# Norm squares on VectorE, later Gelus, deferred gate products and a shifted route in a one-core PEER decoder block

## The chip, the cores and the metric

The kernel runs on one core of a Trainium2 chip. The core has TensorE (PE, with its weight loads PEld), VectorE (DVE), ScalarE (ACT) and GpSimd (POOL), SyncE (SP), which here only issues transfers, and 16 DMA engines that serve all queues. The metric is device time in microseconds (us); lower is better. Times are the median of repeated runs; one further execution was profiled, and all rows of the trace are from that one.

## The reference

The layer is a decoder block on 512 tokens of width 1024, in float32: a mixer of two recurrent head groups, a cross-attention on 256 memory tokens, then a PEER layer, each behind an RMSNorm and added to the stream, and a last RMSNorm. The change lies in the PEER layer and the norm behind it. PEER picks, for each token and each of 8 heads, 16 of 128×128 experts by two sets of 128 keys, and sums the experts' outputs:

```python
def peer_ffn(h, wq, sub_keys, u_table, v_table):
    ...
    q = (hf @ wq).reshape(t, PEER_HEADS, 2, PEER_HALF)
    sc = jnp.einsum('thpd,hpnd->thpn', q, sub_keys).astype(jnp.float32)
    top_v, top_i = lax.top_k(sc, PEER_TOPK)
    ...
    best_v, best_pos = lax.top_k(cand, PEER_TOPK)
    expert_id = jnp.take_along_axis(cand_id, best_pos, axis=-1)
    gate = jax.nn.softmax(best_v, axis=-1)
    ...
    def block(args):
        xb, eb, gb = args
        u = jnp.take(u_table, eb, axis=0)
        act = jax.nn.gelu(jnp.einsum('phkd,pd->phk', u, xb).astype(jnp.float32), approximate=False)
        wgt = (gb * act).astype(v_table.dtype)
        return jnp.einsum('phk,phkd->pd', wgt, jnp.take(v_table, eb, axis=0))
```

So each token uses 128 rows of `u_table` and 128 of `v_table`, of 1024 floats each.

## The kernel before, in words

The 512 tokens are four tiles of 128. The PEER layer is computed in two ways at the same time.

*Gathered tiles* (two tiles, `G0`). `peer_gather` is a generator; each step is one row of work for 128 tokens: POOL gathers one `u` row for each token (`fetch`, L1066, 512 KB), and VectorE multiplies it with the token's vector and sums (L1093). 128 such rows give a tile's 128 activations. A tile's activations then go through Gelu on ScalarE and a product with the gates on VectorE (`weights_`, L1073 and L1074); in the code this is called in the middle of the next 128 rows. Then 128 `v` rows per tile are gathered and added up with those weights (L1104). The order is: 128 `u` rows of the first tile, 128 of the second, 128 `v` rows of the first, 128 of the second, 512 in all, numbered 1 to 512 here. `close` adds the residual to a finished tile, squares it (L1083), takes the norm and returns it for its store; the first tile is closed in the middle of the last 128 rows, the second at the very end. The rows land in a ring of buffers (`buffer`), 14 of them late in the kernel.

*Dense tiles* (two tiles, `G1`). For these all 16384 experts are computed. They are cut into 128 blocks of 128 experts; block e needs 512 KB of each table. For a block, PE multiplies the `u` block with the 256 tokens (L313), ScalarE applies Gelu from PSUM into a room in SBUF (`act_`, L965), VectorE multiplies with the gates of eight blocks at a time (`gated`, L990), and PE multiplies with the `v` block into four PSUM banks that stay open over all blocks (`add`, L993). The `u` side runs 47 blocks ahead (`AHEAD`): 47 blocks are done before the dense loop (`ahead`, called by the letter `a` of the order below), and the other 81 inside it, so at loop step e the activation is that of block e+47. Steps 0 to 80 have both halves, steps 81 to 127 the `v` half alone. The activation's PSUM pool has two banks.

*Gates of the dense tiles.* `route` finds a tile's experts: per head a top 16 of 50 candidates, then the indices are turned by comparisons in float16 (`key`, `at`, `hit`, `prod`). Each `yield` is a step: candidates, eight heads, the rest. `build` then makes, for 16 tokens, the table of gates for all experts: one-hot rows on VectorE (L934), their product with the gates (L938), a product of one-hots on PE (L943), a copy to a staging tile on ScalarE (L944). 14 of 16 groups of the staging tile are stored to DRAM and loaded by POOL later (`gates_of`, L985); the first two groups (`NOW`) are multiplied in place into the activations at once by VectorE (L949). There are 16 builds, eight per dense tile, and three staging tiles.

The order in which the parts are emitted is the string `ORDER_XA`, read from left to right: `p5` runs five steps of the gather, `t2` and `T2` two steps of the route of the first and second dense tile, `b1` and `B1` one build, `a1` one block ahead. 158 gather rows are emitted before the dense loop. In the dense loop `ROWS_BOTH` rows are emitted per step while both halves run and `ROWS_DOWN` afterwards; what is left runs behind the loop. The order of emission isn't the order of an engine's queue: that is set when the program is compiled, by a planner that takes for each engine what its estimate says is ready, the earlier emitted first. Each engine then works its queue strictly in order. Waits between engines are semaphores.

Of the kernel before, what the change touches and what calls it, by code (L numbers as in the profile page):

```python
# [11 lines left out]
AF = mybir.ActivationFunctionType  # L12
OP = mybir.AluOpType
# [15 lines left out]
K = 16  # L29
NSL = PH * K  # L30

ROWS_BOTH, ROWS_DOWN = 3.5, 1.65
NKEY = 128

GSCALE = 2.0 ** 15
# [20 lines left out]
ORDER_XA = ("w2 n0 q008 n1 s0 x0 s1 x1 q104 o0 w1 i0 q148 f0 f1 r6 "  # L56
            "f2 s2 p2 f3 s3 p4 x2 p3 r3 p2 r3 k0 x3 p4 o1 p8 i1 e0 R3 p4 R3 p2 R4 k1 "
            "u0 p5 u1 p5 u2 p5 a1 u3 p5 a2 "
            + "t2 p4 a1 " * 4 + "t2 p4 a9 " + "b1 p5 a1 T2 " * 4 + "b1 p5 a1 T2 a7 d0 " + "b1 p5 a2 " * 3
            + "B1 p5 a1 " * 6 + "a1 p9 B1 p5 B1 p5 a6 ")  # L60


class Phase:
# [12 lines left out]
def _body(ctx, tc, A, out, dbg):  # L76
    from contextlib import ExitStack
    nc = tc.nc
    V, SC, PE, G = nc.vector, nc.scalar, nc.tensor, nc.gpsimd
# [706 lines left out]
    class Peer:  # L786
# [50 lines left out]
        def route_(self, i, spot, hs, PH):  # L837

            tvv = self.tv[i].rearrange("p (a b) c -> p a b c", b=2)[:, hs]
            cand = sct.tile([P, PH, NCAND], F32, name="cand")  # L840
            bv, bi, idf = self.bv[i][:, hs], self.bi[i][:, hs], self.idf[i][:, :, hs]
            tix = self.tix[i][:, 2 * hs.start:2 * hs.stop]
            off = 0
            for a0, n, w in RECT:
                o = cand[:, :, off:off + n * w].rearrange("p h (a b) -> p h a b", a=n)
                G.tensor_tensor(o, tvv[:, :, 0, a0:a0 + n].unsqueeze(3).to_broadcast([P, PH, n, w]),
                                tvv[:, :, 1, 0:w].unsqueeze(2).to_broadcast([P, PH, n, w]), op=OP.add)
                off += n * w
            yield
            for h in range(PH):  # L850
                topk(sct, cand[:, h], bv[:, h], bi[:, h], NCAND)
                yield


            key = sct.tile([P, PH, 2, K], F16, name="key")
            SC.activation(key.rearrange("p a b c -> p (a b) c"), tix, AF.Copy)
            at = sct.tile([P, PH, K], F16, name="at")
            SC.activation(at, bi, AF.Copy)
            step = sct.tile([P, PH, K], F16, name="step")
            V.tensor_copy(step[:, :, 0:1], key[:, :, 0, 0:1])  # L860
            V.tensor_tensor(step[:, :, 1:], key[:, :, 0, 1:], key[:, :, 0, :K - 1], op=OP.subtract)
            hit, prod = (x[:, :PH] for x in spot())
            shape = [P, PH, K, K]

            def over(x):
                return x.unsqueeze(1).to_broadcast(shape)

            def total(out):
                n = K // 2
                while n > 1:  # L870
                    V.tensor_tensor(prod[:, :, :n], prod[:, :, :n], prod[:, :, n:2 * n], op=OP.add)
                    n //= 2
                V.tensor_tensor(out, prod[:, :, 0], prod[:, :, 1], op=OP.add)
            V.tensor_tensor(hit, at.unsqueeze(2).to_broadcast(shape), over(rows_[:, 0]), op=OP.is_ge)
            V.tensor_tensor(prod, hit, step.unsqueeze(3).to_broadcast(shape), op=OP.mult)
            total(idf[:, 0])
            V.tensor_tensor(prod, hit, over(rows_[:, 1]), op=OP.mult)
            first = sct.tile([P, PH, K], F16, name="first")
            total(first)
            V.tensor_tensor(first, at, first, op=OP.subtract)  # L880
            V.tensor_tensor(hit, first.unsqueeze(2).to_broadcast(shape), over(rows_[:, 2]), op=OP.is_equal)
            V.tensor_tensor(prod, hit, key[:, :, 1].unsqueeze(3).to_broadcast(shape), op=OP.mult)
            total(idf[:, 1])
            if self.ids[i] is not None:
                V.scalar_tensor_tensor(self.ids[i][:, hs], idf[:, 0], float(P), idf[:, 1], op0=OP.mult, op1=OP.add)
            yield
# [32 lines left out]
    TG, TS = 16, 8  # L919
    GB = 8  # L920
    NOW = 2
# [5 lines left out]
    def build(t0, bufs, stage, bank):  # L927

        for s in range(0, TG, TS):
            ts = slice(t0 + s, t0 + s + TS)  # L930
            oj, oi, og = hot(bufs())
            key = [slot[:, x, ts].rearrange("p (a q) -> p a q", q=Q).unsqueeze(2) for x in range(2)]
            for o, k in ((oj, key[1]), (oi, key[0])):
                V.tensor_tensor(o, ioq.unsqueeze(1).to_broadcast([P, TS // Q, P, Q]),  # L934
                                k.to_broadcast([P, TS // Q, P, Q]), op=OP.is_equal)
            gates = slot[:, 2:4, ts].rearrange("p g (a q) -> p g a q", q=Q)
            for a in range(TS // Q):
                V.tensor_tensor(og[:, :, a], oi[:, a].unsqueeze(1).to_broadcast([P, 2, P, Q]),  # L938
                                gates[:, :, a].unsqueeze(2).to_broadcast([P, 2, P, Q]), op=OP.mult)
                ps = bank()  # L940
                for k in range(Q):
                    for g in range(2):
                        PE.matmul(ps[:, k], oj[:, a, :, k], og[:, g, a, :, k], start=g == 0, stop=g == 1)  # L943
                SC.activation(stage[:, :, s + a * Q:s + a * Q + Q], ps.rearrange("p t i -> p i t"), AF.Copy, scale=1.0 / GSCALE)  # L944
        nc.scalar.dma_start(gates_[:, :, t0 // TG].rearrange("g p i t -> p g (i t)"),
                            stage[:, NOW * GB:].rearrange("p (g i) t -> p g (i t)", i=GB))
        for g in range(NOW):
            a = room[g][:, :, t0:t0 + TG]
            V.tensor_tensor(a, a, stage[:, g * GB:(g + 1) * GB], op=OP.mult)  # L949

    NHOT = TS * 4 * P

# [6 lines left out]
    room, count_a = [], [0]  # L959
# [102 lines left out]
    def peer_gather(ready, buffer):  # L1062

        def fetch(table, ids, s):
            row = buffer()
            G.indirect_dma_start(out=row, out_offset=None, in_=A[table],  # L1066
                                 in_offset=bass.IndirectOffsetOnAxis(ap=ids[:, s:s + 1], axis=0))
            return row
        late_ = NSL // 2

        def weights_(ti):

            SC.activation(act[ti], act[ti], AF.Gelu)  # L1073
            V.tensor_tensor(act[ti], act[ti], ready[ti], op=OP.mult)  # L1074

        def close(ti):
            hn = first.hn[ti]
            x, wr, junk = buffer(), buffer(), buffer()
            G.dma_start(x, out[ti * P:(ti + 1) * P, :])
            row_(4, wr, G)  # L1080
            V.tensor_tensor(hn, hn, x, op=OP.add)
            ss = sm.tile([P, 1], F32, name="nss")
            SC.activation(junk, hn, AF.Square, accum_out=ss)  # L1083
            V.scalar_tensor_tensor(hn, hn, rstd(ss, 1, "n", 1.0 / D), wr, op0=OP.mult, op1=OP.mult)
            return out[ti * P:(ti + 1) * P, :], hn

        act, done, stored = {}, [], []
        for ti in G0:
            act[ti] = per.tile([P, NSL], F32, name=f"act{ti}", bufs=1)
            hn, ids = first.hn[ti], first.ids[first.tiles.index(ti)].rearrange("p a b -> p (a b)")  # L1090
            for s in range(NSL):
                row = fetch("pu", ids, s)
                V.scalar_tensor_tensor(row, row, 1.0, hn, op0=OP.mult, op1=OP.mult, accum_out=act[ti][:, s:s + 1])  # L1093
                if s == late_ and done:
                    weights_(done.pop())
                yield
            done.append(ti)
        for ti in G0:
            hn, ids = first.hn[ti], first.ids[first.tiles.index(ti)].rearrange("p a b -> p (a b)")
            for s in range(NSL):  # L1100
                row = fetch("pv", ids, s)
                w = act[ti][:, s:s + 1]
                if s:
                    V.scalar_tensor_tensor(hn, row, w, hn, op0=OP.mult, op1=OP.add)  # L1104
                else:
                    V.tensor_scalar(hn, row, w, None, op0=OP.mult)
                if s == late_:
                    if ti == G0[0]:
                        weights_(done.pop())
                    else:  # L1110
                        stored.append(close(G0[0]))
                if s == late_ + 32 and stored:
                    G.dma_start(*stored.pop())
                yield
        G.dma_start(*close(G0[1]))

    mixer(tuple(range(NT)), memory_kv)
# [73 lines left out]
    for what in ORDER_XA.split():  # L1191
# [50 lines left out]
        else:  # L1242
            if kind not in flows:
                i, f = {"r": (0, 0), "R": (1, 0), "t": (0, 0), "T": (1, 0), "b": (0, 1), "B": (1, 1)}[kind]
                g = first if kind in "rR" else second
                flows[kind] = settle(g, g.tiles[i]) if f else g.route(g.tiles[i], spot, 2 if kind == "r" else 1)
            run(flows[kind], n)
    assert count_a[0] == AHEAD
    pe.close()
    pss.close()  # L1250
    wu = pool("wu", 1, side="right")
# [67 lines left out]
```

## Time and profile before

| | us |
|---|---|
| median of 3 runs | 1926.71 (1925.36 to 1937.04) |
| the profiled execution | 1930.96 |
| its span, first to last instruction | 1929.0 |
| PE busy | 1686.6 |
| VectorE busy | 1244.0 |
| GpSimd busy | 839.0 |
| ScalarE busy | 397.8 |

The kernel moves 514.81 MB. A row of the profile's slices cuts the span in 40 parts of 48.2 us; a digit is a tenth of the slice. In the list of waits a line gives the engine and line that waited, for whom, the total, how often, and the longest. A line such as `x40: 383/383/384, 1361.3 to 1629.9` counts instructions of one kind, with shortest, median and longest in ns and the first and last start in us. PE's busy time is that of overlapping records; how fast it goes is read from the distance of starts.

### The profile page before, as it was taken

To read this page: it belongs to the slowest core of one execution; us is meant where nothing else is said; L and a number is where in the kernel's file an instruction comes from. 1 tells how busy PE (TensorE), PEld (TensorE's weight loads), DVE (VectorE), ACT (ScalarE), POOL (GpSimd) and SP (SyncE) were. 2 spreads that over 40 slices of the span, in tenths; PEclk is the share of its full clock that TensorE was granted. 3 is DMA by queue.
4 is the path that set the end of the run, shared out by engine and by line. 5 is a ranking of instruction groups with operands and counts; after the bars stand their busy time and mean duration, and the time that the engine had idled before them with its cause. 6 is when DMAs were issued, how large, how long until landed. Compare 5 with 4: busy or idle time off the path is not lost.

```text
span 1929.0 us, 21360 instructions
## 1 busy us (share of the span) xinstructions
PE 1686.6 (87%) x7444; PEld 1245.9 (65%) x7444; DVE 1244.0 (64%) x2753; ACT 397.8 (21%) x798; POOL 839.0 (43%) x686
## 2 busy tenths in 40 slices
PE   5999999999799978978997699974999999239997
PEld 3878778777788847867886466643666666125443
DVE  5656754662523898997896956668566665797611
ACT  5443442752442222112222100000000000000000
POOL 2122111332210255571543746568566666676500
PEclk9999999999899988998998799986999999669999
DMA  3111111234534678887899999999999999999962
GB/s 133 61 55 55 45 50 56 66 112 150 178 118 147 230 278 305 321 322 254 298 357 350 345 385 410 410 410 392 410 410 409 410 410 410 403 408 410 409 208 87
DMA packets 165355, 514.81 MB, mean 267 GB/s; under 512 B 15616, under 2 KB 44416, under 8 KB 163456
## 3 DMA queue, kind: packets, MB, share of 16 engines
q0 software_dynamic: 76608, 286.30, 38.3%
q1 hardware_dynamic: 59712, 212.48, 30.2%
q10 hardware_dynamic: 28928, 14.68, 2.6%
q8 instruction: 58, 0.95, 0.2%
q14 instruction: 49, 0.40, 0.1%
HBM read 494.52 MB, written 18.87 MB: 266 GB/s over the span
## 4 chain that ended last, share of the span: by engine, by line
PE 42%; DMA 26%; DVE 20%; issue 5%; POOL 4%; ACT 2%; DVEq 0%; SPq 0%; POOLq 0%; ACTq 0%
PE o L993 9%; PE pj L271 7%; DMA row<-in_pv,ids 7%; PE pj L313 6%; PE pj L284 6%; PE acc L445 4%; DMA W<-in_pv,ids 3%; DVE dh L1104 3%; PE acc L943 3%; DVE W L1093 2%; DMA wl<-in_pu,ids 2%; DMA row<-in_pu,ids 2%; DMA W<-in_pu,ids 2%; DMA Vm<-in_pu,ids 2%; DMA KT<-in_pv,ids 2%
## 5 line engine op out<-in xcount | busy, mean ns | idle before, releaser
L313 PE MATMUL pa<-dh,ld 128*128 128x256 f32 x1296 | 299.5, 385 | 105.2 <-ACT dh L965 104.6
L993 PE MATMUL o<-ld,W 128*128 128x512 f32 x832 | 369.9, 595 | 2.1 <-DVE W L949 1.1
L313 PEld LDWEIGHTS pa<-dh,ld 128*128 128x128 f32 x1296 | 250.2, 194 | 174.1 <-ACT dh L965 106.3
L993 PEld LDWEIGHTS o<-ld,W 128*128 128x128 f32 x832 | 158.9, 191 | 174.1 <-issue 167.4
L221 POOL TENSOR_TENSOR wl<-w,wh 128x1024 fp32r<-128x1024 f32 x38 | 92.4, 2434 | 343.9 <-ACT wh L236 289.7
L313 PE MATMUL pj<-dh,w 128*128 128x256 f32 x704 | 167.8, 393 | 4.5 <-ACT W L965 4.5
L313 PEld LDWEIGHTS pj<-dh,w 128*128 128x128 f32 x704 | 137.1, 199 | 23.2 <-ACT W L965 4.9
L1066 POOL DMA_INDIRECT W<-in_pu,ids x71 | 94.4, 1329 | 97.1 <-DVE W L1093 44.5
L1066 POOL DMA_INDIRECT row<-in_pu,ids x74 | 97.4, 1316 | 83.1 <-DVE row L1093 36.9
L1104 DVE SCALAR_TENSOR_TENSOR dh<-row,act,dh 128x1024 f32<-128x1024 f32 x72 | 92.5, 1284 | 57.2 <-DMA row<-in_pv,ids 56.4
L1066 POOL DMA_INDIRECT row<-in_pv,ids x74 | 99.7, 1348 | 47.0 <-DMA W<-in_pv,ids 20.1
L313 PE MATMUL pj<-dh 128*128 128x256 f32 x496 | 111.4, 380 | 1.8 <-ACT W L965 1.8
L1093 DVE SCALAR_TENSOR_TENSOR row<-row,dh 128x1024 f32<-128x1024 f32 x74 | 89.1, 1220 | 36.3 <-DMA row<-in_pu,ids 36.0
L284 PE MATMUL pj<-hT,wh 128*128 128x512 f32 x320 | 110.9, 418 | 0.0
L965 ACT ACTIVATE W<-pa 128x256 f32<-128x256 f32 x65 | 24.9, 383 | 401.9 <-PE pa L313 396.4
L271 PE MATMUL pj<-wh,hT 128*128 128x512 f32 x320 | 106.3, 405 | 0.4 <-ACT hT L211 0.4
L313 PEld LDWEIGHTS pj<-dh 128*128 128x128 f32 x496 | 93.7, 191 | 14.3 <-ACT W L965 2.2
L1093 DVE SCALAR_TENSOR_TENSOR W<-W,dh 128x1024 f32<-128x1024 f32 x71 | 86.0, 1222 | 15.5 <-DMA W<-in_pu,ids 15.4
L993 PE MATMUL o<-ld,dh 128*128 128x512 f32 x192 | 85.2, 593 | 0.0
L236 ACT ACTIVATE wh<-w 128x1024 fp32r<-128x1024 f32 x56 | 59.3, 1058 | 124.7 <-PE pj L271 64.1
L1066 POOL DMA_INDIRECT wh<-in_pu,ids x41 | 64.3, 1567 | 33.2 <-DVE wh L1093 8.5
L1066 POOL DMA_INDIRECT wl<-in_pu,ids x42 | 49.8, 1186 | 66.1 <-DVE tv L783 18.6
(431 smaller groups left out, 3090.3 us busy)
## 6 DMA issues: line engine op xcount, KB each, us to landing
ld<-in_pv SPq DMA_DIRECT2D x128, 512.0 KB, 6.8
ld<-in_pt SPq DMA_DIRECT2D x81, 512.0 KB, 6.8
gates__132<-W ACTq DMA_DIRECT2D x16, 896.0 KB, 12.3
W<-gates__132 POOLq DMA_DIRECT2D x14, 1024.0 KB, 17.4
w<-in_pt SPq DMA_DIRECT2D x24, 512.0 KB, 6.8
dh<-in_pt SPq DMA_DIRECT2D x23, 512.0 KB, 6.9
w<-in_win SPq DMA_DIRECT2D x20, 512.0 KB, 3.6
w<-in_pwq SPq DMA_DIRECT2D x16, 512.0 KB, 4.0
```

Of the source, the lines that this page charges most:

```text
L221: G.tensor_tensor(out, a, hi, op=OP.subtract)
L236: SC.activation(hi, wt, AF.Copy)
L271: PE.matmul(acc[i], a[:, d, i * P:(i + 1) * P], b[:, z], start=d == 0 and m == 0, stop=d == DB - 1 and m == len(pairs) - 1)
L284: PE.matmul(acc[:, :n * P], a[:, d], b[:, d], start=d == 0 and m == 0, stop=d == DB - 1 and m == 2)
L313: PE.matmul(ps, w[:, d], h[:, d], start=d == 0, stop=d == DB - 1)
L445: PE.matmul(ps[:, i], l[:, i], r[:, i], start=True, stop=True)
L943: PE.matmul(ps[:, k], oj[:, a, :, k], og[:, g, a, :, k], start=g == 0, stop=g == 1)
L965: SC.activation(place(e), ps, AF.Gelu)
L993: PE.matmul(outs[DENSE[i]][z], place(e)[:, i * P:(i + 1) * P], v[:, z * 512:(z + 1) * 512], start=e == 0, stop=e == NKEY - 1)
L1066: G.indirect_dma_start(out=row, out_offset=None, in_=A[table], in_offset=bass.IndirectOffsetOnAxis(ap=ids[:, s:s + 1], axis=0))
L1093: V.scalar_tensor_tensor(row, row, 1.0, hn, op0=OP.mult, op1=OP.mult, accum_out=act[ti][:, s:s + 1])
L1104: V.scalar_tensor_tensor(hn, row, w, hn, op0=OP.mult, op1=OP.add)
```

## The change

It has six edits, which keep the computation.

1. `close` squares on VectorE (an operation with a running sum) in place of ScalarE's Square.
2. `weights_` is called at the 121st row of the next 128 rows in place of the 65th; `close` of the first tile stays at the 65th.
3. `build` hands its two products for the first two groups to a list, and the next build runs them in its second half, between the one-hots and their products with the gates. The last is run behind the order string.
4. `route_` converts the indices and positions to float16 on VectorE in place of ScalarE.
5. In the order string two steps of the second dense tile's route and four gather rows stand ahead of the first build; the later ones move up, and a `p9` near the end becomes `p5`.
6. `ROWS_BOTH` is 3.15 in place of 3.5, `ROWS_DOWN` 2.3 in place of 1.65.

```diff
-ROWS_BOTH, ROWS_DOWN = 3.5, 1.65
+ROWS_BOTH, ROWS_DOWN = 3.15, 2.3
...
-            + "t2 p4 a1 " * 4 + "t2 p4 a9 " + "b1 p5 a1 T2 " * 4 + "b1 p5 a1 T2 a7 d0 " + "b1 p5 a2 " * 3
-            + "B1 p5 a1 " * 6 + "a1 p9 B1 p5 B1 p5 a6 ")
+            + "t2 p4 a1 " * 4 + "t2 p4 a9 T2 p4 " + "b1 p5 a1 T2 " * 4 + "b1 p5 a8 d0 " + "b1 p5 a2 " * 3
+            + "B1 p5 a1 " * 6 + "a1 p5 B1 p5 B1 p5 a6 ")
...
-            SC.activation(key.rearrange("p a b c -> p (a b) c"), tix, AF.Copy)
+            V.tensor_copy(key.rearrange("p a b c -> p (a b) c"), tix)
             at = sct.tile([P, PH, K], F16, name="at")
-            SC.activation(at, bi, AF.Copy)
+            V.tensor_copy(at, bi)
...
             gates = slot[:, 2:4, ts].rearrange("p g (a q) -> p g a q", q=Q)
+            while s and fresh:
+                fresh.pop()()
             for a in range(TS // Q):
...
-        for g in range(NOW):
-            a = room[g][:, :, t0:t0 + TG]
-            V.tensor_tensor(a, a, stage[:, g * GB:(g + 1) * GB], op=OP.mult)
+
+        def apply():
+            for g in range(NOW):
+                a = room[g][:, :, t0:t0 + TG]
+                V.tensor_tensor(a, a, stage[:, g * GB:(g + 1) * GB], op=OP.mult)
+        fresh.append(apply)
+
+    fresh = []
...
-        late_ = NSL // 2
+        late_, later = NSL // 2, NSL - 8
...
-            SC.activation(junk, hn, AF.Square, accum_out=ss)
+            V.scalar_tensor_tensor(junk, hn, 1.0, hn, op0=OP.mult, op1=OP.mult, accum_out=ss)
...
-                if s == late_ and done:
+                if s == later and done:
                     weights_(done.pop())
...
-                if s == late_:
-                    if ti == G0[0]:
-                        weights_(done.pop())
-                    else:
-                        stored.append(close(G0[0]))
+                if s == later and ti == G0[0]:
+                    weights_(done.pop())
+                if s == late_ and ti != G0[0]:
+                    stored.append(close(G0[0]))
...
     assert count_a[0] == AHEAD
+    fresh.pop()()
     pe.close()
```

## The prediction

> **What bounds the kernel now.** I read the page first (busy time, slices), then a table of stretches, then the waits inside the stretches where PE falls idle, then ScalarE in order of time.
>
> ```profile
> span 1929.0 us, 21360 instructions
> PE   5999999999799978978997699974999999239997
> PEclk9999999999899988998998799986999999669999
> GB/s 133 61 55 55 45 50 56 66 112 150 178 118 147 230 278 305 321 322 254 298 357 350 345 385 410 410 410 392 410 410 409 410 410 410 403 408 410 409 208 87
> ...
> 620.00:864.00 244.00, 214.29 (x964) 175.04 (x962) 222.06 (x944) 46.03 (x109) 123.41 (x118) 0.94 0.79 285
> 885.00:1108.00 223.00, 188.82 (x1061) 162.13 (x1060) 188.17 (x380) 53.26 (x102) 102.47 (x72) 0.91 0.90 316
> ...
> 1288.00:1327.00 39.00, 0.71 (x2) 0.00 (x0) 34.68 (x56) 0.50 (x3) 30.20 (x25) 0.55 1.02 404
> 1327.00:1638.00 311.00, 310.87 (x1076) 207.02 (x1077) 192.17 (x149) 17.59 (x47) 203.48 (x154) 0.99 1.02 408
> 1638.00:1720.00 82.00, 15.94 (x54) 9.76 (x52) 69.08 (x54) 1.33 (x4) 58.74 (x54) 0.62 1.02 406
> 1754.00:1845.00 91.00, 91.00 (x214) 40.41 (x213) 58.07 (x56) 1.53 (x3) 47.83 (x36) 1.00 1.00 396
> 1845.00:1929.00 84.00, 73.84 (x173) 32.44 (x171) 8.47 (x22) 2.89 (x8) 0.54 (x1) 0.97 0.38 123
> ...
> 1632.00:1929.00 297.00, 220.63 (x571) 110.19 (x570) 171.04 (x168) 8.03 (x20) 135.29 (x115) 0.88 0.84 323
> ```
>
> A window row gives its stretch, its length, busy time of PE, PEld, DVE, ACT and POOL (with counts), the granted clock, the DMA share and GB/s. From 1108 us to 1845 us DMA moves about 400 to 410 GB/s whatever PE does: that stage is DMA's. After 1845 us DMA is nearly empty (123 GB/s) while PE is still busy 73.84 of 84 us. So PE arrives late at the end, with work that could have run earlier, beside full transfers. It lost that time in two holes, 1288 to 1327 and 1638 to 1720, where it was idle while DMA ran on. Before 1108 us DMA is not full, and VectorE is the busiest of what remains: 222.06 of 244 and 188.17 of 223 us.
>
> The waits in the two holes:
>
> ```profile
> ACT act L1073 <- DVE row L1093: 54.6, 1, 54.6
> PE pa L313 <- ACT dh L965: 38.4, 1, 38.4
> ...
> ACT row L1083 <- DVE dh L1081: 81.5, 1, 81.5
> PE pa L313 <- ACT dh L965: 66.2, 1, 66.2
> ...
> 1052.73 0.30 ACT L1073 ACTIVATE act<-act 128x128 f32<-128x128 f32 x1
> 1058.77 0.38 ACT L965 ACTIVATE W<-pa 128x256 f32<-128x256 f32 x1
> ...
> L965 ACT ACTIVATE W<-pa x25: 383/383/383, 1058.8 to 1257.8; 128x256 f32<-128x256 f32 x25
> L965 ACT ACTIVATE dh<-pa x2: 383/383/383, 1264.7 to 1271.5; 128x256 f32<-128x256 f32 x2
> ...
> L965 ACT ACTIVATE W<-pa x40: 383/383/384, 1361.3 to 1629.9; 128x256 f32<-128x256 f32 x40
> L965 ACT ACTIVATE dh<-pa x7: 365/383/384, 1326.7 to 1636.8; 128x256 f32<-128x256 f32 x7
> ...
> L965 ACT ACTIVATE dh<-pa x7: 363/383/383, 1719.7 to 1754.1; 128x256 f32<-128x256 f32 x7
> ...
> 600.00:1637.00 1037.00, 549.15 (x407) 0.94 0.93 353
> 600.00:1718.60 1118.60, 605.74 (x456) 0.91 0.94 357
> ```
>
> ScalarE works its queue in order. The square of the first gathered tile's norm (L1083) stands in it behind 74 of the 81 dense activations (25+2+40+7), and can't run before VectorE has reached row 449 of the 512 gathered rows. PE runs on to that point at 6.89 us a block ((1629.9−1361.3)/39), but the rows come more slowly: only 407 had been issued at 1637 us. So ScalarE stood 81.5 us for the square, the next activations stood behind it, the two PSUM banks stayed full, and PE lost 66.2 us. The first hole is the same with the Gelu of the second tile's activations (L1073), which needs row 256 and stands behind 27 dense activations.
>
> The last two rows, and those below of the gathers, are windows of L1066 alone, in which x counts rows issued. The queue orders aren't those of the source: the first L1073 is emitted at row 193, some ten blocks into the dense loop (158 rows stand ahead of it), but ran at 1052.73 us, ahead of the first dense activation; the second is emitted at row 321, block 46, and ran behind block 26. An activation goes where the planner of the program thought its input ready.
>
> **The change part by part.** The rows of the end come first: PE's last stretch, and the closing of the second gathered tile.
>
> ```profile
> 1835.58 83.27 PE o L993 x194
> ...
> 1839.81 1.23 DVE L1081 TENSOR_TENSOR dh<-dh,W 128x1024 f32<-128x1024 f32 x1 [1.12 <-DMA W<-out]
> 1844.56 1.28 DVE L1084 SCALAR_TENSOR_TENSOR dh<-dh,nr,W 128x1024 f32<-128x1024 f32 x1
> 1846.14 0.54 POOL L1115 DMA_DIRECT2D out<-dh  x1 [19.74 <-DVE dh L1084]
> DMA to landing us min/median/max: 3.6/3.6/3.6
> ```
>
> *The square on VectorE.* The add before it and the norm after it are VectorE's, so nothing of another engine waits any more, and no dense activation stands behind it. It costs VectorE one operation for each of the two tiles, like the scaling behind it (1.28 us); in the last stage VectorE waits for rows, which hides it. With the 66.2 us gone, PE's last matmul, which ended at 1918.85, would end at about 1853. What is late next is DMA: from 1632 us the rest of the program moved 297 us × 323 GB/s = 95.9 MB, which at 410 GB/s takes 234 us, to 1866 us. The gathered rows now end last, and behind the last one stands that closing: 1839.8 to the store's landing at 1849.7 is 10 us; PE's own tail (1918.85 to 1929.0) is 10 us too. So DMA's side ends at 1876 and PE's at 1863: the span becomes 1876, **−53 us**. If DMA were no limit it would be −66; if the 410 GB/s sank to the 396 of the row 1754:1845, 242 us and −45.
>
> A page reads otherwise: the Trainium skill's "DMA: Bandwidth & Descriptors", section Specifications, gives about 358 GB/s as the HBM limit of a core. By it the 95.9 MB would take 268 us and the gain of this part would be 19 us; the trace differs, with 410 GB/s in most slices behind the 24th, and the measurement decides.
>
> *Functions 120 rows late.* The Gelu's source place moves 56 rows back; its input is ready at row 128 or 256 as before. As the trace shows it placed by readiness, I take it to stay where it is: the 38.4 us hole remains, and 0. That is affordable: with it PE still ends 13 us ahead of DMA. If the Gelu moves back instead, PE runs 38 us further ahead and the end, DMA's, is the same. Its reader, the product with the gates, is needed by row 257 or 385; the new place is eight rows ahead of that.
>
> *Built gates applied later.*
>
> ```profile
> DVE W L949 <- ACT W L944: 28.4, 13, 12.2
> ...
> DVE wl L1093 <- DMA wl<-in_pu,ids: 4.1, 1, 4.1
> ```
>
> Between 885 and 1108 us VectorE is idle 35 us, 28.4 of them in front of the two products of a build, waiting for ScalarE's copy out of PSUM; one wait is 12.2 us, the other twelve 1.35 us on average. An apply that comes half a build later finds its data there. The copies stay ahead of it on ScalarE; the staging tile is held longer, but there are three. What can take the gain back is PE (188.82 of the 223 us) and DMA (316 GB/s on average, slices at 357): 28.4 us less would need 316×223/194.6 = 362 GB/s. Bounds: −28 and 0; I take half, **−14**.
>
> *Key and position copies on VectorE.*
>
> ```profile
> ACT at L858 <- DVE bi L784: 26.3, 5, 17.3
> POOL row L1066 <- ACT at L858: 6.0, 1, 6.0
> L871 DVE TENSOR_TENSOR wh<-wh 128x256 f16<-128x256 f16 x6 | 1.7, 290 | 0.1
> ```
>
> Five routes, two copies each: ten of about 0.26 us (by the L871 row of the larger one's size), 2.6 us on a busy VectorE. In return ScalarE no longer stands for VectorE (26.3 us at the position copy alone), and the one gather that waited 6.0 us for that doesn't. Between +3 and −6; **−1**.
>
> *Part of the last route ahead of the builds, and four rows with it.* Two steps of the route (the candidates on POOL, one head's top 16 on VectorE) and four rows come before the first build, and four rows fewer near the end: 158 rows stand ahead of the dense loop either way. VectorE does the same work. 0, with ±5 for the other order.
>
> *3.15 and 2.3 rows a block.* POOL's queue holds only gathers and gate loads there:
>
> ```profile
> 600.00:1672.70 1072.70, 571.57 (x424) 0.93 0.93 355
> ...
> 1344.00:1632.00 288.00, 182.97 (x133) 1.00 1.03 410
> ...
> 1586.10 2.28 DVE L990 TENSOR_TENSOR W<-W,W 128x2048 f32<-128x2048 f32 x1
> ```
>
> The last gate load ran after 424 rows, its source place (158 + 76×3.5); it moves to 397. It needs the buffer of three groups before, whose product VectorE runs at 1586 us; some 383 rows had been issued then (407 less 51 us of 133 in 288). VectorE is at most 14 buffers behind POOL, so when POOL comes to row 397, VectorE is at 383 or later, past that product. So no wait is added, by a narrow margin; one row costs 2 us. The rows themselves come at DMA's pace, 133 in 288 us (3.2 a block), not at the source's 3.5. 0.
>
> Sum: 53+14+1 = 68 us off the profiled execution's 1930.96: 1863. The median of the runs is 4 us below that execution, so 1859; I say 1860.
>
> **The rivals.**
>
> *The Gelu becomes PE's bound.* Behind row 256 PE has a fixed rest, ending at 1853 with 27 blocks done. If the new plan puts the Gelu earlier by k blocks, PE ends 6.89k us later and passes DMA's end from k = 2. At k = 2 to 6 the span is 1877 to 1904, less 15 from the builds and with the 2 us around the span 1864 to 1891. For it: the orders are planned anew; against: rows ahead of the dense loop stay 158.
>
> *The same, slower than before.* At k = 15, the wait at block 12, PE ends at 1956 and the span is 1966, less 15 and with the 2 us around the span 1953: 1.1% over 1931. From there on the change loses by over 1%. It would have to stand less than half as far into the loop as now. Little speaks for that.
>
> *Another wait takes the square's place.* When PE isn't held at block 74, it might be at a product of the gates in VectorE's queue, or by its loads. For it: PE would run ahead of the rows again, as it did before both holes; against: from 1344 to 1632 PE never waited beside the same transfers, and the products stand some 35 blocks ahead of their use. If it takes all back: about 1912, the builds' part alone.
>
> *The builds give nothing, or the new order costs there.* The square's part alone: 1931−53 = 1878, 1874 against the median; with +15 of new stalls 1889.
>
> **How the numbers follow.** Forecast (square and some of the builds, 1840 to 1872): 0.58. Builds give nothing or cost: 0.17. Gelu bound: 0.13. Another wait takes it back: 0.08. Slower: 0.04. The page's 358 GB/s would give 1926.7−19−15 = 1893; after such rows it gets no chance of its own. About 1% (19 us) is what a measurement of this kernel can tell from no change. The first three cases are faster by over 1%: 0.86 with a little of the fourth; same 0.10, slower 0.04. The range, 1838 to 1893, holds the first three but for their edges.
>
> **What would show it.** Right: no wait of ScalarE at the square's line, no hole of PE behind the first, DMA at 400 or more until the last 15 us, and the last instructions those of the gathered tile's store. In the builds: no wait at the apply line, and the last build over by about 1093 instead of 1108 us. Wrong: a hole of PE between 1640 and 1720 with another name, PE alone at the end for tens of us, or a Gelu wait much over 55 us.

## The result, and the profile after

| | before | after |
|---|---|---|
| median, us | 1931.88 (1925.36 to 1937.88, 4 runs) | 1861.43 (1859.21 to 1870.93, 4 runs) |
| ratio | | 0.9639, interval 0.9603 to 0.9675 |
| the profiled execution, us | 1930.96 | 1863.43 |

The change takes 70 us off (3.6%, with an interval of 3.2 to 4.0%). The forecast was 1860 us, in a range of 1838 to 1893. Between the profiled executions the forecast was 68 us, and 67.5 were measured. The median came out 1.4 us above the forecast. That it is so near is luck: its terms were off by more than that, in opposite directions, as is shown below. One run of the experiment E3 below (7774 us) and one of the kernel before (9650 us) lie far outside all others and count in no ratio.

The page of the changed kernel first: span, PE's slices, GB/s, and the shares of the chain that ended last (from the last instruction back, what held it at each step). The last line is the same chain in the kernel before.

```profile
span 1861.5 us, 21345 instructions
PE   4999999999799986996998979993899999999993
GB/s 138 63 57 35 57 40 46 69 102 149 168 88 162 149 261 269 350 335 372 259 332 408 367 385 410 410 410 410 410 410 410 409 410 409 410 409 409 409 411 257
DMA 38%; PE 33%; DVE 19%; issue 4%; POOL 3%; ACT 2%; SPq 0%; DVEq 0%; POOLq 0%; ACTq 0%
```

```profile
PE 42%; DMA 26%; DVE 20%; issue 5%; POOL 4%; ACT 2%; DVEq 0%; SPq 0%; POOLq 0%; ACTq 0%
```

PE's share of that chain falls from 42% to 33% and DMA's rises from 26% to 38%. In PE's slices the second gap (the digits 2 and 3 near the end of the row before) is gone; the first (the 3 in the 28th slice) has stayed. DMA now runs at 409 to 411 GB/s in every slice from the 25th to the 39th, so to within 47 us of the end, where before it fell to 208 and 87 in the last two. By the Trainium skill's "DMA: Bandwidth & Descriptors", section Specifications, a core's HBM limit is about 358 GB/s; the trace shows 410 over 15 slices of 46.5 us, so the 1893 us that the prediction worked out from it fall.

The waits of the dense loop, in the changed kernel (engine and line that waited, for whom, total, times, longest):

```profile
ACT ld L1057 <- DVE ld L1056: 184.7, 1, 184.7
ACT act L1080 <- DVE row L1100: 50.4, 1, 50.4
PE pa L313 <- ACT dh L972: 34.2, 1, 34.2
```

The wait of 81.5 us at the square isn't there, and PE's 66.2 us behind it aren't either. The Gelu's wait and the first hole have stayed, 4 us shorter each. The 184.7 us are ScalarE's at the end: it has no work left between the last dense activation and the dense tiles' closing.

Windows of the changed kernel, in the columns of the prediction's:

```profile
885.00:1108.00 223.00, 200.95 (x1095) 169.81 (x1094) 197.62 (x403) 53.70 (x103) 112.90 (x82) 0.94 0.97 348
1108.00:1843.50 735.50, 687.72 (x2204) 419.58 (x2202) 477.45 (x473) 29.66 (x78) 471.69 (x358) 0.97 1.02 408
1843.50:1862.00 18.50, 0.00 (x0) 0.00 (x0) 12.87 (x37) 2.56 (x8) 0.54 (x1) 0.50 0.22 85
```

Ahead of the dense loop DMA moves 348 GB/s in place of 316, and PE is busy 201 us in place of 189 of the same 223. Then DMA is full for 735 us. PE has nothing left to do in the last stretch. The timeline of that end:

```profile
1814.74 15.18 PE L1000 MATMUL o<-ld,dh 128*128 128x512 f32 x35
...
1827.64 2.61 DVE L1111 SCALAR_TENSOR_TENSOR dh<-KT,act,dh 128x1024 f32<-128x1024 f32 x2 [0.43 <-DMA KT<-in_pv,ids]
1830.28 2.61 DVE L1111 SCALAR_TENSOR_TENSOR dh<-Vm,act,dh 128x1024 f32<-128x1024 f32 x2
1832.92 5.25 DVE L1111 SCALAR_TENSOR_TENSOR dh<-row,act,dh 128x1024 f32<-128x1024 f32 x4
...
1842.17 1.28 DVE L1111 SCALAR_TENSOR_TENSOR dh<-wl,act,dh 128x1024 f32<-128x1024 f32 x1
1843.49 1.22 DVE L1088 TENSOR_TENSOR dh<-dh,W 128x1024 f32<-128x1024 f32 x1
1844.74 1.22 DVE L1090 SCALAR_TENSOR_TENSOR KT<-dh 128x1024 f32<-128x1024 f32 x1
...
1848.32 1.28 DVE L1091 SCALAR_TENSOR_TENSOR dh<-dh,nr,W 128x1024 f32<-128x1024 f32 x1
1849.52 2.48 DVE L1056 TENSOR_TENSOR ld<-o,ld 128x512 f32<-128x512 f32 x4
1849.90 0.54 POOL L1121 DMA_DIRECT2D out<-dh  x1 [14.90 <-DVE dh L1091]
...
1855.45 2.74 DVE L1066 SCALAR_TENSOR_TENSOR ld<-ld,f0r 128x512 f32<-128x512 f32 x4
1856.23 2.32 SPq L1067 DMA_DIRECT2D out<-ld  x4
```

PE ends at 1829.9, and the last gathered row is added by 1843.5. Behind it stand not one closing but two, in series on VectorE: the gathered tile's (L1088 to L1091, with the square at L1090, 1.22 us), and then the dense tiles' (L1056 to L1066). The dense closing had its last input from PE at 1829.9, 20 us before it starts: it stands behind the last rows and the gathered closing in VectorE's queue. From the last row to the end of the span it is 18 us. The last twelve rows are added back to back, from 1827.64 to 1843.45, one per 1.32 us, where a row of 0.524 MB takes 1.28 us at 410 GB/s. So at the very end VectorE's adds pace the rows as much as DMA does; no run here tells the two apart.

### The profile page after: what moved, and what is told of

Read it like the earlier page. It is cut to its first block, busy times and chain, and to the rows that moved or that the text cites. A ratio compares the mean times of both kernels' runs of the same rounds, so it can differ in the third digit from the quotient of the medians.

```text
span 1861.5 us, 21345 instructions
## 1 busy us (share of the span) xinstructions
PE 1682.0 (90%) x7444; PEld 1240.6 (67%) x7444; DVE 1248.2 (67%) x2767; ACT 393.9 (21%) x784; POOL 849.9 (46%) x686
## 4 chain that ended last, share of the span: by engine, by line
DMA 38%; PE 33%; DVE 19%; issue 4%; POOL 3%; ACT 2%; SPq 0%; DVEq 0%; POOLq 0%; ACTq 0%
PE pj L313 7%; PE pj L271 7%; DMA row<-in_pv,ids 7%; PE pj L284 6%; DMA W<-in_pv,ids 6%; DMA Vm<-in_pv,ids 5%; PE acc L445 4%; DMA row<-in_pu,ids 3%; DMA wl<-in_pv,ids 3%; DMA W<-gates__132 3%; PE acc L945 2%; DMA gates__132<-W 2%; DVE W L1100 2%; DMA wl<-in_pu,ids 2%; DMA KT<-in_pv,ids 1%
## 5 line engine op out<-in xcount | busy, mean ns | idle before, releaser
L313 PE MATMUL pa<-dh,ld 128*128 128x256 f32 x1296 | 295.5, 381 | 34.7 <-ACT dh L972 34.2
L313 PE MATMUL pj<-dh,w 128*128 128x256 f32 x704 | 161.3, 383 | 0.0
L1073 POOL DMA_INDIRECT wl<-in_pu,ids x41 | 56.6, 1380 | 49.1 <-DVE tv L783 18.6
L1073 POOL DMA_INDIRECT wh<-in_pu,ids x40 | 54.2, 1354 | 49.9 <-DVE wh L1100 22.3
```

The lines of the kernel that those rows point to most:

```text
L313: PE.matmul(ps, w[:, d], h[:, d], start=d == 0, stop=d == DB - 1)
```

## The experiments

Theory A is the prediction's: ScalarE's wait at the square held PE; once that is gone the rows, and so DMA, end last; the builds' products gain about half their wait; the other edits do next to nothing. The rivals differ by experiment and are named in each expectation. Each ratio is against runs of the kernel before on the same chip, whose medians were 1933.23 to 1935.04 us.

**E1, E2: the square alone, and the changed kernel without it.** In E1 the first line below replaces the second in the kernel before; E2 is the reverse in the changed kernel.

```diff
+            V.scalar_tensor_tensor(junk, hn, 1.0, hn, op0=OP.mult, op1=OP.mult, accum_out=ss)
-            SC.activation(junk, hn, AF.Square, accum_out=ss)
```

> The kernel before with edit 1 alone (norm squares on VectorE). Theory A (PE was held at the square behind block 74, and DMA is what is late next): the 66 us hole goes, PE runs on, the gathered rows end last; 1932 - 53 = 1879 us, 1870 to 1888, and the last products of a build still wait some 28 us. Rival B (the gain of the whole change comes from the rows per block, 3.15 and 2.3): 1932 us, the hole turns up under another name.

Measured: 1889.49 us, ratio 0.9803 (0.976 to 0.9847), so 38 us with an interval of 30 to 46. That is 1.5 us above theory A's range, and far from rival B's 1932. PE's only wait from 1200 us on in E1:

```profile
PE pa L313 <- ACT dh L965: 38.3, 1, 38.3
```

> The changed kernel with the square back on ScalarE. Theory A: the square stands behind block 74 or so again and waits for row 449; PE gets a second hole of 60 us or so and ends alone; 1861 + 45 to 53 = 1906 to 1916 us. Rival B: the rows per block keep the hole away, 1861 to 1870 us.

Measured: 1910.49 us, ratio 0.9905 (0.9874 to 0.9936), 49 us above the changed kernel. The waits of the dense loop in E2:

```profile
PE pa L313 <- ACT dh L972: 99.8, 2, 65.6
ACT row L1090 <- DVE dh L1088: 80.9, 1, 80.9
```

With the square back on ScalarE, its wait (80.9 us) and PE's second hole (65.6) return. In E1 both are gone (the 38.3 us are the first hole), and this is its only edit. So this wait held PE. E1's end, in its timeline:

```profile
1849.61 4.88 PE L993 MATMUL o<-ld,dh 128*128 128x512 f32 x11
...
1866.68 1.28 DVE L1104 SCALAR_TENSOR_TENSOR dh<-wl,act,dh 128x1024 f32<-128x1024 f32 x1
1874.04 2.48 DVE L1049 TENSOR_TENSOR ld<-o,ld 128x512 f32<-128x512 f32 x4
```

PE ends at 1854.5 (forecast about 1853), and the last row is added by 1868.0 (forecast 1866, DMA's end): both within 2 us. The span ends at 1886.0, 18 us later, where the forecast had 10. The profiled gain is 1929.0−1886.0 = 43 us; of the 10 us short of 53, 8 are the tail and 2 the last row.

**E3, E4: the builds' products half a build later, alone and taken back.**

```diff
+            while s and fresh:
+                fresh.pop()()
...
+        def apply():
...
+        fresh.append(apply)
...
+    fresh.pop()()
```

> The kernel before with edit 3 alone (a build's two products half a build later). Theory A: VectorE's 28 us of waits there go to under 5, the builds end about 15 us sooner, all behind them moves up, 1932 - 15 = 1917 us, 1908 to 1925. Rival: the builds are held by PE or DMA, or what is won is lost in the holes, 1928 to 1936 us.

Measured: 1915.78 us, ratio 0.9928 (0.9899 to 0.9957): 14 us, interval 8 to 20.

> The changed kernel with the two products of a build at once again. Theory A: the wait of some 28 us at them is back, 1861 + 15 = 1876 us, 1868 to 1884. Rival: no part in the gain, 1857 to 1866 us.

Measured: 1883.92 us, ratio 0.9773 (0.9718 to 0.9828), 22 us above the changed kernel. VectorE's wait at the product, in E4, and below it in E3:

```profile
DVE W L949 <- ACT W L944: 29.4, 13, 12.8
```

```profile
DVE W L953 <- ACT W L946: 1.1, 1, 1.1
```

The wait, 28.4 us before, goes to 1.1, and about half of it reaches the end when the edit is alone. In the changed kernel it is worth 22 of the 28 by the medians.

**E5: Gelu and product called at row 121 in place of 65, alone** (edit 2 as in the diff of the change).

> The kernel before with edit 2 alone (Gelu and product called at row 121 in place of 65). Theory A (a queue's place is set by when the input is ready, not by the call): the second Gelu still stands behind about 27 dense activations, both holes stay, 1932 us, 1926 to 1938. Rival C: the call's place counts, the first hole goes, and PE, which ends alone in the kernel before, gains up to 38 us: 1894 to 1915.

Measured: 1934.29 us, ratio 1.001 (0.9986 to 1.0035): nothing. ScalarE's second Gelu in E5's timeline, and below it the dense activations that ran ahead of it:

```profile
1318.40 0.31 ACT L1073 ACTIVATE act<-act 128x128 f32<-128x128 f32 x1 [53.58 <-DVE row L1093]
```

```profile
L965 ACT ACTIVATE W<-pa x25: 383/383/384, 1050.9 to 1250.7; 128x256 f32<-128x256 f32 x25
...
L965 ACT ACTIVATE dh<-pa x2: 383/383/383, 1257.6 to 1264.4; 128x256 f32<-128x256 f32 x2
```

It stands behind the same 25+2 dense activations as before, though it is emitted 56 rows later. In ScalarE's queue its place isn't that of its call.

**E6, E7, E8: the rows per block, the copies, the order, each alone** (edits 6, 4 and 5). In E7 two lines change:

```diff
-            SC.activation(key.rearrange("p a b c -> p (a b) c"), tix, AF.Copy)
+            V.tensor_copy(key.rearrange("p a b c -> p (a b) c"), tix)
...
-            SC.activation(at, bi, AF.Copy)
+            V.tensor_copy(at, bi)
```

> The kernel before with edit 6 alone (3.15 and 2.3 rows per block). Theory A: GpSimd's queue only gets its gate loads some rows sooner, the rows go on at the pace of DMA, both holes stay, 1932 us, 1924 to 1940. Rival B: 1880 to 1910 us.

Measured: 1929.04 us, ratio 0.9964 (0.9932 to 0.9996): 7 us, interval 1 to 13, barely more than nothing.

> The kernel before with edit 4 alone (key and position copies on VectorE). Theory A: -1 us, between 3 slower and 6 faster: 1926 to 1935. Rival: ScalarE's freed waits (key 50 us, positions 26 us) let PE and the builds run up, 1905 to 1925.

Measured: 1922.16 us, ratio 0.9938 (0.9905 to 0.9971): 12 us, interval 6 to 18. This lies outside theory A's range and inside the rival's (1905 to 1925), which had named ScalarE's freed waits. The prediction's 1 us is the first term found wrong.

> The kernel before with edit 5 alone (two route steps and four rows ahead of the first build). Theory A: nothing, 1927 to 1937 us. Rival: the route ends sooner and the second half of the builds with it, 1910 to 1925.

Measured: 1927.29 us, ratio 0.9978 (0.9949 to 1.0007): 4 us, not told from nothing. In all of E3 and E5 to E8 PE keeps both holes, 99.7 to 104.7 us in two waits, against 104.6 before: no other edit takes the second hole away.

**E9: the changed kernel without its first hole.** To take the wait away, the second Gelu itself is left out.

```diff
-            SC.activation(act[ti], act[ti], AF.Gelu)
+            if ti == G0[0]:
+                SC.activation(act[ti], act[ti], AF.Gelu)
```

> The changed kernel without the Gelu of the second gathered tile's activations (left out of the computation; the product with the gates stays). Theory A (DMA sets the end, the first hole costs nothing): PE's hole of 34 us goes, PE ends its blocks some 30 us sooner, and the time stays, 1856 to 1866 us. Rival D (the hole is a loss of its own): 1825 to 1840 us.

Measured: 1866.59 us, ratio 0.9654 (0.9586 to 0.9722): not told from the changed kernel (0.9639), and clear of rival D. The waits of its dense loop:

```profile
PE o L1000 <- DVE dh L997: 31.3, 1, 31.3
```

The hole of 34.2 us behind the Gelu is gone, and PE, now further ahead of the rows, stands 31.3 us at a product of the gates in VectorE's queue instead. PE's idle time has moved: PE ends at 1822.4, only 7 us sooner than the changed kernel's 1829.9, not the 30 expected. DMA is as full as it was (408 GB/s from 1108 to 1836.5 us). So taking this hole away gains nothing.

**E10, E11: sixteen rows fewer at the end,** in the changed kernel and in the kernel before: the last 16 gathered rows of the second tile are left out.

```diff
-            for s in range(NSL):
+            for s in range(NSL if ti == G0[0] else NSL - 16):
                 row = fetch("pv", ids, s)
```

> The changed kernel with the last 16 rows of the second gathered tile left out (its sum lacks 16 experts). Theory A: the gathered rows are last, 16 x 0.524 MB at 410 GB/s are 20.5 us less, 1841 us, 1836 to 1848. Rival E (PE's blocks are still last): 1856 to 1863 us.

Measured: 1845.34 us, ratio 0.9515 (0.945 to 0.958), 16 us less than the changed kernel by the medians, 24 by the ratios. Sixteen rows are 8.4 MB, 20 us at 410 GB/s.

> The kernel before with the same 16 rows left out. Theory A: PE's blocks are last there and nothing of PE is changed, 1933 us, 1926 to 1938, within a few us. Rival E (the rows set the end of the kernel before too): 1910 to 1916 us.

Measured: 1931.64 us, ratio 0.9995 (0.9962 to 1.0027): nothing. So the rows end last in the changed kernel, and did not in the kernel before. How little there is behind them shows in E10's timeline:

```profile
1819.68 17.33 PE L1000 MATMUL o<-ld,dh 128*128 128x512 f32 x40
```

PE ends at 1837.0 and the span at 1847.2: with 16 rows fewer PE is last again. A cut of the rows alone has about 14 us to give, by the two profiled spans (1861.5 and 1847.2).

**E12: the copies back on ScalarE, in the changed kernel,** to size E7's surprise a second time.

> The changed kernel with the key and position copies back on ScalarE. Alone, edit 4 took 12 us off the kernel before where 1 was forecast. Theory F (ScalarE, freed of its waits for VectorE, lets the stage before the dense loop run faster): 1861 + 8 to 14 = 1869 to 1875 us, and the last gate product some 10 us later than in the changed kernel. Rival G (the 12 us were in good part the scatter of that stage from run to run): 1858 to 1866 us.

Measured: 1881.88 us (1869.2 to 1890.88, 6 runs), ratio 0.9733 (0.9697 to 0.9769). Against the changed kernel's 0.9639 that is 0.0094 of 1932 us: 18 us, give or take 10 by the two intervals. ScalarE's waits from 620 to 1100 us, in E12:

```profile
ACT at L858 <- DVE bi L784: 23.3, 4, 16.9
ACT key L856 <- DVE tix L784: 21.7, 3, 11.9
...
ACT key L856 <- DVE W L882: 16.7, 1, 16.7
```

62 us of ScalarE's standing come back with the copies; in the changed kernel ScalarE has no wait at these lines. The median lies above theory F's range (1869 to 1875), so F had the direction right and the size too small, though its 8 to 14 us lie within 18 give or take 10. Rival G is out: no run was below 1869.2.

What is worked ahead shows in the stretches 600 to 885 and 885 to 1108 us of E12, and in the first of them in the changed kernel (its second is above):

```profile
600.00:885.00 285.00, 244.50 (x1113) 201.35 (x1112) 245.97 (x1032) 52.47 (x124) 134.03 (x127) 0.92 0.77 283
885.00:1108.00 223.00, 192.69 (x1058) 163.39 (x1057) 194.03 (x387) 53.04 (x102) 106.03 (x76) 0.92 0.95 339
```

```profile
600.00:885.00 285.00, 246.92 (x1134) 203.37 (x1133) 243.37 (x1027) 51.23 (x117) 132.12 (x127) 0.93 0.79 287
```

By 1108 us PE has run 58 matmuls more in the changed kernel, with 10.7 us more busy time, and VectorE about the same (441.0 against 440.0 us). The last gate product ends at 1092.3 in place of 1098.5 us: 6 us sooner, where theory F had 10. ScalarE doesn't stand less for it; its standing moves. From 600 to 1108 us its waits for VectorE add up to 112 us in E12 and 76 in the changed kernel, its waits for PE to 270 and 303. PE's waits for ScalarE in the same stretch add up to 37.0 and 27.4 us, and to 34.3 in the kernel before and 23.3 in E7, some 10 us less both times. The largest one, in E12 and in the changed kernel:

```profile
PE acc L945 <- ACT W L946: 15.3, 1, 15.3
```

```profile
PE acc L945 <- ACT W L946: 5.7, 1, 5.7
```

This fits the path of the rival in E7: PE gets its PSUM copies earlier from a ScalarE that no longer stands for VectorE. It was not isolated, and the profiled spans differ by 5.9 us where the ratios have 18. So the runs show that the copies gain 12 to 18 us; the path is argued, not shown.

## Why the prediction came out right, point by point

- **The square: mechanism right, tail mis-sized.** The step was "DMA's side ends at 1876 and PE's at 1863: the span becomes 1876", −53. E1 measured 38 by its ratio and 43 in its profile. PE's and the rows' ends were right within 2 us. Wrong was the tail, "1839.8 to the store's landing at 1849.7 is 10 us": it was taken from the kernel before, where the gathered closing ran while PE still worked and the dense closing ran alone after it. Once the rows end last, both stand in series on VectorE, 18 us. So the last instructions aren't those of the gathered tile's store, as the prediction's signs had it, but the dense tiles'. The term that the prediction sized at 10 measured 18.
- **The later functions: right.** E5 measured nothing, the Gelu kept its place, and E9 shows that nothing is gained by taking its hole away.
- **The builds: right.** −14 in the prediction, −14 alone; in the changed kernel −22, inside the bound of 28. The last build was over at 1092.3 us, about as said.
- **The copies: the term that failed.** "Between +3 and −6; −1" measured −12 alone and −18 in the changed kernel. The step priced what VectorE takes on (ten short operations) and the one gather that waited, and gave the rest of ScalarE's standing no price. The waits at both lines added up to 76.8 us before; the prediction quoted only the 26.3 of them at the position copy.
- **Order and rows per block: 0 in the prediction**; 4 and 7 us, of which only the second is told from nothing, and barely. No new wait at a gate load appeared: the longest for a buffer is 4.8 us, against 4.7 before.

How the errors met: the forecast put the last row of the full change at 1866−15 = 1851 and the span's end 10 us later, at 1861. Measured were 1843.5 and 1861.5. The row came 8 us earlier and the tail was 8 us longer. For the earlier row, half can be traced: ahead of the loop DMA moved (348−316)×223 us and (287−284)×285 us more, 8.0 MB in all, 19.5 us at 410 GB/s where the forecast had 15. (The 284 are the kernel before's, below; the other three stand in rows shown.)

```profile
600.00:885.00 285.00, 242.42 (x1092) 199.49 (x1091) 242.49 (x1025) 51.28 (x122) 134.91 (x128) 0.92 0.79 284
```

The single edits add up to 38+14+12+7+4−2 = 73 us, against 70 for the whole. Undone one at a time from the changed kernel the profiles give 39.7 (square, 1901.2−1861.5), 22.6 (products, 1884.1) and 5.9 us (copies, 1867.4), together 68; the medians give 49, 22 and 20, which is more than the whole. Those were timed in other series than the changed kernel, and runs of one kernel spread over some 8 to 25 us, so these sizes hold to some 10 us. Only the square is clearly the largest; the products and the copies aren't told apart by the medians.

The rivals: the Gelu didn't move (E5, and the changed kernel's own waits). Another wait of PE did come when it got further ahead (E9: 31.3 us at L997), which is the mechanism of the rival "another wait takes the square's place", but only behind a PE that was 34 us earlier still. That the builds give nothing was excluded by E3 and E4. One sum of the prediction is off: its first three cases add up to 0.88, not to the 0.86 that it gives for faster by over 1%.

## What to carry to other kernels

When a wait goes, work out the tail again for the engine that is now late: what ran beside other work before may stand in series on one queue afterwards, here 18 us in place of 10. A wait in an in-order queue is to be priced by all that stands behind it, not by the engine's idle share: ScalarE was busy 21% of the span, and taking ten small copies out of its queue still gained 12 us alone. And a hole of an engine cost nothing here while the resource that ends last was full beside it; leave out what makes the hole before spending work on it.

## What the hardware showed unexpectedly

The same copy of 128x256 elements from uint32 to float16 takes VectorE a third less than ScalarE. The lines of E7 and, below, of the kernel before:

```profile
L856 DVE CAST key<-tix x5: 214/270/279, 644.1 to 933.7; 128x256 f16<-128x256 uint32 x3, 128x128 f16<-128x128 uint32 x2
```

```profile
L856 ACT ACTIVATE key<-tix x5: 309/416/417, 634.6 to 866.1; 128x256 f16<-128x256 uint32 x3, 128x128 f16<-128x128 uint32 x2
```

The medians are of the larger shape, 270 against 416 ns. And the gathers of 4 KB rows together with the plain loads of the tables held 409 to 411 GB/s for some 700 us, whatever PE, VectorE and ScalarE did beside them, and in E9 with PE's idle time at another place.
